# Two-layer fp32 trunk on one core: the split of the weights into high and low parts, done on a whole loaded tile instead of one 128-row chunk

## The chip, the core and the metric

One NeuronCore of a Trainium2 chip runs the whole program in one launch. The metric is device time in microseconds (us); lower is better. The engines named below are PE (the matrix engine; PEld is its weight load, which overlaps it), DVE (the vector engine), ACT (the scalar engine), POOL and SP (whose queue issues most transfers from memory).

## The reference

Two layers over 256 tokens of width 2048, all in fp32. Layer 0 mixes a differential attention with a gated delta rule, layer 1 is a dilated attention, and each is followed by a squared-ReLU MLP. Cut to what matters here:

```python
D_MODEL = 2048
SEQ = 256
D_FF = 4 * D_MODEL
...
def rms_norm(x, g):
    xf = x.astype(jnp.float32)
    y = xf * lax.rsqrt(jnp.mean(xf * xf, axis=-1, keepdims=True) + NORM_EPS)
    return (y * g.astype(jnp.float32)).astype(x.dtype)
...
def squared_relu_mlp(h, w1, w2):
    return jnp.square(jax.nn.relu(h @ w1)) @ w2
...
    proj = h @ w_in
...
    return o @ w_out
```

The time goes into the products with the large weights: `w_in` and `w_out` of both mixers, and `w1` (2048 x 8192) and `w2` (8192 x 2048) of both MLPs.

## The kernel before

**The large products.** `dense()` computes one output block, 256 tokens by up to 512 columns, in two PSUM tiles of 128 tokens. It walks over the contracted dimension in chunks of 128 rows, 16 for a full block. Each operand is held as the sum of a high and a low part, both of the type `F32R`, and each chunk costs three products for each token half: high by high (L206), high by the weights' low part (L207), and low by the weights' high part (L208). That is six matmuls of 128x128 by 128x512 to a chunk.

**The weights' way.** `wload` (L171) has SP's queue load two chunks at once into a raw tile `wr` of 128 x 2 x 512 fp32 (4 buffers). For each chunk ACT copies its half of the raw tile to the high part `wh` (L201, a cast), and DVE subtracts the high part from the raw half to get `wl` (L202, which the profile shows at L107, the line of the helper `tt`). `wh` and `wl` are each 128 x 512 and come from a pool with 6 buffers, so that up to six split chunks exist at a time. A name such as `n_3h<-n_3r` is the high part of block 3 of the product n, made from its raw tile; `n_3l` is the low part.

**What sets the order.** The engines run in order. Which instruction stands where on each engine is decided by a tile scheduler from priorities: an instruction normally has the place in which the program issues it, and `tc.high_priority(offset=AHEAD)` with AHEAD = 60 puts the two instructions of a split 60 places earlier. After a chunk `drip()` takes a step or two of the side work, which lies in three streams of generators: attention and delta rule, norms, transposes.

**The stages.** Layer 0's mixer runs from 0 to about 509 us with products such as b0 to b3 (delta rule inputs), z0 to z2 (gates, 264 columns wide), a and v blocks, and `wo`. MLP 0 follows to about 1216 us, layer 1's mixer (products c and cv; heads' side work e1 to e7) to about 1601 us, then MLP 1. An MLP works in 4 groups. In each it makes four products m_0 to m_3 (x times `w1`), each followed by ReLU and square on ACT, 16 block transposes on DVE (L289), a cast `hh` on ACT (L314) and a subtraction `hl` on DVE, both 128 x 1024. Then come four products n_0 to n_3 with `w2`, which take `hh` and `hl` as stationary operands. So the first chunks of n_0 that need m_3's `hh` and `hl` come twelve chunks after m_3's last matmul, and there are 8 such passages from m_3 to n_0.

**The start.** The first three raw tiles of b0 are loaded between the pieces of x. ACT scales the transposed pieces of x (`xa0h`, L123), DVE makes their low parts (`xa0l`, L113), and b0's first splits stand between these.

## Time and profile before

| | us |
|---|---|
| median of 3 runs | 2316.6 |
| the runs | 2315.55, 2316.6, 2317.71 |
| span of the profiled execution, first to last instruction | 2313.0 |
| PE busy | 2298.6 |
| DVE busy | 1733.1 |
| ACT busy | 1275.1 |

The profiled execution is known by its span, which lies 3.6 us under the median of the runs. A busy time is the sum over the instructions of an engine, so it shows how much of the span an engine was not idle, and neither how fast it worked nor what it waited for. Idle time is listed with what released the engine from it: in a row, `[1.12 <-ACT b0h L201]` says that the engine had been idle for 1.12 us until ACT's instruction on b0h of line 201 ended. A row `x2` is two instructions in a row of the same form, with their joint time. The granted clock of PE was 1.000 of full speed in the whole span.

### The profile page before, as it was taken

What the parts mean: (1) busy time and instruction counts of PE and PEld (TensorE: products, weight loads), DVE (VectorE), ACT (ScalarE), POOL (GpSimd) and SP (SyncE); (2) the same over time, 40 slices, a digit from 0 to 9 for tenths busy, and PEclk for the clock granted to TensorE, in tenths of its full rate; (3) what the DMA queues carried; (4) which work ended last, traced back from release to release, by engine and by line L of the source; (5) the groups of instructions that cost most, each with busy time, mean ns of one, the idle gap of its engine ahead of it and who ended that gap; (6) DMA issues with size and microseconds to landing.
All of it is one profiled execution on the core that took longest, in us unless ns stands there. A gap on an engine that the chain in (4) does not pass through costs nothing.

```text
span 2313.0 us, 31488 instructions
## 1 busy us (share of the span) xinstructions
PE 2298.6 (99%) x10536; PEld 1889.0 (82%) x10536; DVE 1733.1 (75%) x3539; ACT 1275.1 (55%) x2376; POOL 5.6 (0%) x15
## 2 busy tenths in 40 slices
PE   9999999999999999999999999999999999999999
PEld 8888888788888888888888888888888888888887
DVE  7758778867757757857898888987875775775774
ACT  6656665655545545545555555556554554554553
POOL 0000000000000000000000000000000000000000
PEclk9999999999999999999999999999999999999999
DMA  8655454556566666665656555555656656656564
GB/s 264 174 170 166 149 174 143 166 180 190 192 188 183 202 186 186 202 188 186 198 183 200 172 166 176 171 175 181 190 193 189 192 191 190 192 191 189 185 209 155
DMA packets 264775, 426.65 MB, mean 184 GB/s; under 512 B 22514, under 2 KB 94372, under 8 KB 264612
## 3 DMA queue, kind: packets, MB, share of 16 engines
q1 hardware_dynamic: 255812, 420.04, 57.7%
q10 hardware_dynamic: 8800, 4.60, 0.8%
q8 instruction: 82, 1.34, 0.2%
q14 instruction: 81, 0.66, 0.1%
HBM read 420.11 MB, written 4.46 MB: 184 GB/s over the span
## 4 chain that ended last, share of the span: by engine, by line
PE 88%; DVE 8%; DMA 2%; ACT 1%; issue 1%; SPq 0%; ACTq 0%; DVEq 0%
PE n_0p L208 3%; PE n_2p L207 3%; PE n_1p L207 3%; PE n_1p L208 3%; PE n_2p L206 3%; PE n_1p L206 3%; PE n_2p L208 3%; PE n_0p L207 3%; PE n_0p L206 3%; PE n_3p L208 3%; PE n_3p L207 3%; PE n_3p L206 3%; PE m_0p L206 3%; PE m_0p L207 3%; PE m_0p L208 3%; PE m_3p L208 3%
## 5 line engine op out<-in xcount | busy, mean ns | idle before, releaser
L107 DVE TENSOR_TENSOR n_3l<-n_3r,n_3h 128x512 fp32r<-128x512 f32 x128 | 88.5, 692 | 73.0 <-ACT n_3h L201 72.6
L107 DVE TENSOR_TENSOR n_2l<-n_2r,n_2h 128x512 fp32r<-128x512 f32 x128 | 88.4, 692 | 73.0 <-ACT n_2h L201 72.6
L107 DVE TENSOR_TENSOR m_0l<-m_0r,m_0h 128x512 fp32r<-128x512 f32 x128 | 88.5, 692 | 68.0 <-ACT m_0h L201 67.8
L201 ACT CAST n_3h<-n_3r 128x512 fp32r<-128x512 f32 x128 | 79.3, 621 | 94.8 <-PE n_3p L208 59.4
L201 ACT CAST n_2h<-n_2r 128x512 fp32r<-128x512 f32 x128 | 79.3, 620 | 94.8 <-PE n_2p L208 59.4
L107 DVE TENSOR_TENSOR n_1l<-n_1r,n_1h 128x512 fp32r<-128x512 f32 x128 | 87.0, 691 | 55.0 <-ACT n_1h L201 54.8
L201 ACT CAST m_0h<-m_0r 128x512 fp32r<-128x512 f32 x128 | 79.6, 622 | 83.8 <-DVE m_0l L107 39.8
L201 ACT CAST n_1h<-n_1r 128x512 fp32r<-128x512 f32 x128 | 78.6, 620 | 81.7 <-PE n_1p L208 59.4
L201 ACT CAST m_1h<-m_1r 128x512 fp32r<-128x512 f32 x128 | 78.1, 622 | 64.7 <-PE m_1p L208 35.3
L107 DVE TENSOR_TENSOR m_1l<-m_1r,m_1h 128x512 fp32r<-128x512 f32 x128 | 87.1, 691 | 33.7 <-ACT m_1h L201 32.0
L201 ACT CAST n_0h<-n_0r 128x512 fp32r<-128x512 f32 x128 | 77.4, 619 | 48.5 <-PE n_0p L208 37.1
L201 ACT CAST m_3h<-m_3r 128x512 fp32r<-128x512 f32 x128 | 77.1, 621 | 46.8 <-PE m_3p L208 35.3
L201 ACT CAST m_2h<-m_2r 128x512 fp32r<-128x512 f32 x128 | 76.9, 621 | 46.8 <-PE m_2p L208 35.3
L107 DVE TENSOR_TENSOR n_0l<-n_0r,n_0h 128x512 fp32r<-128x512 f32 x128 | 84.9, 689 | 11.3 <-ACT n_0h L201 9.6
L107 DVE TENSOR_TENSOR m_3l<-m_3r,m_3h 128x512 fp32r<-128x512 f32 x128 | 84.9, 689 | 11.3 <-ACT m_3h L201 9.6
L107 DVE TENSOR_TENSOR m_2l<-m_2r,m_2h 128x512 fp32r<-128x512 f32 x128 | 84.9, 689 | 11.2 <-ACT m_2h L201 9.5
L289 DVE STREAM_TRANSPOSE m_0hT<-m_0r 32x256 f32<-32x256 f32 x128 | 55.8, 436 | 10.5 <-ACT m_0r L123 8.0
L289 DVE STREAM_TRANSPOSE m_1hT<-m_1r 32x256 f32<-32x256 f32 x128 | 55.8, 436 | 10.4 <-ACT m_1r L123 7.9
L289 DVE STREAM_TRANSPOSE m_2hT<-m_2r 32x256 f32<-32x256 f32 x128 | 55.8, 436 | 10.4 <-ACT m_2r L123 7.9
L289 DVE STREAM_TRANSPOSE m_3hT<-m_3r 32x256 f32<-32x256 f32 x128 | 55.8, 436 | 10.4 <-ACT m_3r L123 7.9
L208 PE MATMUL n_0p<-n_0h,m_3hl 128*128 128x512 f32 x64 | 25.8, 403 | 0.0
L207 PE MATMUL n_0p<-n_0l,m_2hh 128*128 128x512 f32 x64 | 25.3, 396 | 0.0
(2552 smaller groups left out, 7405.7 us busy)
## 6 DMA issues: line engine op xcount, KB each, us to landing
m_0r<-in_mlp_w_dram SPq DMA_DIRECT2D x64, 512.0 KB
m_1r<-in_mlp_w_dram SPq DMA_DIRECT2D x64, 512.0 KB
m_2r<-in_mlp_w_dram SPq DMA_DIRECT2D x64, 512.0 KB
m_3r<-in_mlp_w_dram SPq DMA_DIRECT2D x64, 512.0 KB
n_0r<-in_mlp_w_dram SPq DMA_DIRECT2D x64, 512.0 KB
n_1r<-in_mlp_w_dram SPq DMA_DIRECT2D x64, 512.0 KB
n_2r<-in_mlp_w_dram SPq DMA_DIRECT2D x64, 512.0 KB
n_3r<-in_mlp_w_dram SPq DMA_DIRECT2D x64, 512.0 KB
```

The source lines that it names most:

```text
L107: V.tensor_tensor(out=o, in0=a, in1=b, op=op)
L201: S.copy(wh, w)
L206: E.matmul(o, lhsT=sh, rhs=wh, start=kc == first, stop=False)
L207: E.matmul(o, lhsT=sh, rhs=wl, start=False, stop=False)
L208: E.matmul(o, lhsT=sl, rhs=wh, start=False, stop=kc == last)
L289: V.transpose(out=dv[:, :, :, q], in_=sv[:, :, :, j, :])
```

## The change

The split of the weights works on the whole raw tile. At every second chunk one ACT cast makes the high part of both chunks, 128 x 2 x 512, and one DVE subtraction the low part; the six matmuls of each chunk read their half of these tiles. `wh` and `wl` have twice the size and half as many buffers (3 instead of 6), so that they take the same memory. The two instructions of a pair stand in the program where those of its first chunk stood, with the same offset of 60. Comments and docstrings are taken out; lines after the split are numbered one higher (L207 to L209 for the matmuls).

```diff
-    wp = ctx.enter_context(tc.tile_pool(name="wp", bufs=6))
+    wp = ctx.enter_context(tc.tile_pool(name="wp", bufs=3))
...
             if j % 2 == 0:
                 raw = pre[j // 2] if j // 2 < len(pre) else wload(wsrc, kc, nm)
-            w = raw[:, j % 2, :n]
-            wh = wp.tile([P, 512], F32R, tag="wh", name=f"{nm}h{kc}")[:, :n]
-            wl = wp.tile([P, 512], F32R, tag="wl", name=f"{nm}l{kc}")[:, :n]
-            with tc.high_priority(offset=AHEAD):
-                S.copy(wh, w)
-                tt(wl, w, wh.bitcast(F32), ALU.subtract)
+                w = raw[:, :, :n]
+                wh2 = wp.tile([P, 2, 512], F32R, tag="wh", name=f"{nm}h{kc}")[:, :, :n]
+                wl2 = wp.tile([P, 2, 512], F32R, tag="wl", name=f"{nm}l{kc}")[:, :, :n]
+                with tc.high_priority(offset=AHEAD):
+                    S.copy(wh2, w)
+                    tt(wl2, w, wh2.bitcast(F32), ALU.subtract)
+            wh, wl = wh2[:, j % 2], wl2[:, j % 2]
             for h in range(NH):
                 sh, sl = stat(kc, h)
                 o = ps[h][:, :n]
```

In the program as built, ACT has 792 instructions fewer and DVE 792 fewer; PE has the same matmuls and transposes, in an order that differs only within layer 0's mixer. Three places follow, before and after; the number at the end of a name tells buffers apart, and the width is at the end of a row.

ACT at the start of the program, before: b0's casts (L201) stand between the activations that scale x's pieces and sum its squares.

```order
L123 ACTIVATE xa0h<-xa0t_132,gt 128x256
L201 CAST b0h_225<-b0r_108 128x512
L201 CAST b0h_235<-b0r_108 128x512
L123 ACTIVATE xa0h<-xa0t_132,gt 128x256
L123 ACTIVATE xa0h<-xa0t_141,gt 128x256
L125 ACTIVATE xas0j_247,ssqp<-xq_100 128x512
L125 ACTIVATE xas1j_269,ssqp<-xq_101 128x512
L123 ACTIVATE xa0h<-xa0t_141,gt 128x256
L201 CAST b0h_249<-b0r_112 128x512
L123 ACTIVATE xa1h<-xa1t_152,gt 128x256
L201 CAST b0h_259<-b0r_112 128x512
```

The same place after:

```order
L123 ACTIVATE xa0h<-xa0t_132,gt 128x256
L201 CAST b0h_225<-b0r_108 128x1024
L123 ACTIVATE xa0h<-xa0t_132,gt 128x256
L123 ACTIVATE xa0h<-xa0t_141,gt 128x256
L125 ACTIVATE xas0j_243,ssqp<-xq_100 128x512
L125 ACTIVATE xas1j_261,ssqp<-xq_101 128x512
L201 CAST b0h_245<-b0r_112 128x1024
L123 ACTIVATE xa0h<-xa0t_141,gt 128x256
L123 ACTIVATE xa1h<-xa1t_152,gt 128x256
```

The first two casts became one, and the second pair's cast now stands ahead of the last piece of `xa0h` and the first of `xa1h`.

DVE around a passage from m_3 to n_0, before (m_0_3 is group 0, block 3; the layer's number is left out): transposes of m_3's result, the subtractions for n_0's weights, and the subtraction `m_0_3hl` that n_0's last chunks need.

```order
L289 STREAM_TRANSPOSE m_0_3hT<-m_0_3r 32x2x4x32 x2
L107 TENSOR_TENSOR n_0_0l_6812<-n_0_0r_6809,n_0_0h_6811 128x512
L289 STREAM_TRANSPOSE m_0_3hT<-m_0_3r 32x2x4x32 x2
L107 TENSOR_TENSOR n_0_0l_6822<-n_0_0r_6809,n_0_0h_6821 128x512
L289 STREAM_TRANSPOSE m_0_3hT<-m_0_3r 32x2x4x32 x3
L107 TENSOR_TENSOR n_0_0l_6834<-n_0_0r_6831,n_0_0h_6833 128x512
L289 STREAM_TRANSPOSE m_0_3hT<-m_0_3r 32x2x4x32 x2
L107 TENSOR_TENSOR n_0_0l_6844<-n_0_0r_6831,n_0_0h_6843 128x512
L107 TENSOR_TENSOR m_0_3hl<-m_0_3hT,m_0_3hh 128x1024
L107 TENSOR_TENSOR n_0_0l_6856<-n_0_0r_6853,n_0_0h_6855 128x512
```

The same place after:

```order
L290 STREAM_TRANSPOSE m_0_3hT<-m_0_3r 32x2x4x32 x4
L107 TENSOR_TENSOR n_0_0l_6012<-n_0_0r_6009,n_0_0h_6011 128x1024
L290 STREAM_TRANSPOSE m_0_3hT<-m_0_3r 32x2x4x32 x5
L107 TENSOR_TENSOR n_0_0l_6034<-n_0_0r_6031,n_0_0h_6033 128x1024
L290 STREAM_TRANSPOSE m_0_3hT<-m_0_3r 32x2x4x32 x4
L107 TENSOR_TENSOR n_0_0l_6056<-n_0_0r_6053,n_0_0h_6055 128x1024
L290 STREAM_TRANSPOSE m_0_3hT<-m_0_3r 32x2x4x32 x3
L107 TENSOR_TENSOR n_0_0l_6074<-n_0_0r_6071,n_0_0h_6073 128x1024
L107 TENSOR_TENSOR m_0_3hl<-m_0_3hT,m_0_3hh 128x1024
L107 TENSOR_TENSOR n_0_0l_6092<-n_0_0r_6089,n_0_0h_6091 128x1024
```

Between two subtractions there are now three to five transposes instead of two or three, and `m_0_3hl` still has one subtraction between it and the last transposes.

ACT in layer 0's mixer during the product z1, before: casts of z1's chunks, 264 columns wide, and the copies `c3x` (L543) of the transposes `c3t` that PE makes for the convolution.

```order
L201 CAST z1h_3243<-z1r_3241 128x264
L201 CAST z1h_3257<-z1r_3241 128x264
L201 CAST z1h_3269<-z1r_3267 128x264
L543 COPY c3x<-c3t_3197 128x2x256
L201 CAST z1h_3292<-z1r_3267 128x264
L123 ACTIVATE qk_3194<-c3x,cw 128x256
L543 COPY c3x<-c3t_3203 128x2x256
```

The same place after:

```order
L201 CAST z1h_2852<-z1r_2850 128x2x264
L201 CAST z1h_2885<-z1r_2883 128x2x264
L201 CAST z1h_2903<-z1r_2901 128x2x264
L544 COPY c3x<-c3t_2865 128x2x256
L544 COPY c3x<-c3t_2871 128x2x256
L123 ACTIVATE qk_2862<-c3x,cw 128x256
L201 CAST z1h_2925<-z1r_2923 128x2x264
```

Three casts, one for each of the three buffers, stand ahead of the copies, and the copies now stand together.

## Rows read from the trace of the kernel before

**Rows 1.** The page's first part: busy time, share of the span and instructions of each engine.

```profile
PE 2298.6 (99%) x10536; PEld 1889.0 (82%) x10536; DVE 1733.1 (75%) x3539; ACT 1275.1 (55%) x2376; POOL 5.6 (0%) x15
```

**Rows 2.** Busy time of each engine by stage: the start, layer 0's mixer, MLP 0, layer 1's mixer, MLP 1. Columns: the stretch, its length, busy us and instructions of each engine, PE's granted clock, share of the DMA engines' time, GB/s.

```profile
0.00:30.00 30.00, 27.20 (x128) 22.32 (x129) 20.07 (x66) 20.98 (x51) 1.20 (x6) 1.00 0.81 264
30.00:460.00 430.00, 426.50 (x2282) 355.85 (x2281) 337.28 (x952) 273.53 (x665) 4.38 (x9) 1.00 0.56 170
...
509.00:1216.00 707.00, 707.00 (x3083) 578.16 (x3082) 521.36 (x893) 372.97 (x608) 0.00 (x0) 1.00 0.61 190
1216.00:1601.00 385.00, 380.58 (x1744) 315.53 (x1743) 326.01 (x748) 216.28 (x416) 0.00 (x0) 1.00 0.55 177
1601.00:2309.00 708.00, 708.00 (x3083) 577.55 (x3081) 494.77 (x830) 362.91 (x580) 0.00 (x0) 1.00 0.60 189
```

**Rows 3.** What PE waited for, over the span: us in total, number of waits, the longest. The first two rows shown are the first and the last of three alike (e3pt, e1pt, e5pt). The last row is the smallest that the view lists.

```profile
PE e3pt L231 <- DVE e3sm L117: 1.5, 1, 1.5
...
PE e5pt L231 <- DVE e5sm L117: 1.5, 1, 1.5
...
PE c3t L231 <- ACT c3x L543: 0.9, 1, 0.9
...
PE g0lp L705 <- DMA g0xy<-scx: 0.2, 1, 0.2
```

**Rows 4.** The timeline in MLP 0, in the product n_3 (first and seventh matmul of the block), around the end of n_2 on ACT and DVE, and in m_2. Columns: start, us, engine, line, operation, out and in, shape, idle before and its releaser.

```profile
664.68 0.40 PE L206 MATMUL n_3p<-n_3h,m_0hh 128*128 128x512 f32 x1
...
666.08 0.40 PE L206 MATMUL n_3p<-n_3h,m_0hh 128*128 128x512 f32 x1
...
735.40 0.39 PE L206 MATMUL m_2p<-m_2h,xb0h 128*128 128x512 f32 x1
...
736.76 0.39 PE L206 MATMUL m_2p<-m_2h,xb1h 128*128 128x512 f32 x1
...
666.28 0.62 ACT L201 CAST n_3h<-n_3r 128x512 fp32r<-128x512 f32 x1 [0.77 <-PE n_3p L208]
...
664.13 0.69 DVE L107 TENSOR_TENSOR n_3l<-n_3r,n_3h 128x512 fp32r<-128x512 f32 x1 [0.71 <-ACT n_3h L201]
```

**Rows 5.** Busy time in two stretches of MLP 0: the products n_1 to n_3 of group 0, and m_1 to m_3 of group 1; each is three blocks of 16 chunks, 288 matmuls. Columns as in rows 2.

```profile
619.88:687.08 67.20, 67.20 (x290) 54.05 (x288) 36.58 (x55) 29.82 (x48) 0.00 (x0) 1.00 0.61 193
708.88:774.16 65.28, 65.28 (x289) 54.07 (x288) 55.96 (x100) 38.18 (x61) 0.00 (x0) 1.00 0.60 187
```

**Rows 6.** Prices of one instruction: two of the page's costliest groups (busy us, mean ns of one, idle before and what ended it), and the 128x1024 cast and subtraction in the views of the tiles m_0hh and m_0hl (duration in ns, least, median and most, first and last start).

```profile
L107 DVE TENSOR_TENSOR n_3l<-n_3r,n_3h 128x512 fp32r<-128x512 f32 x128 | 88.5, 692 | 73.0 <-ACT n_3h L201 72.6
...
L201 ACT CAST n_3h<-n_3r 128x512 fp32r<-128x512 f32 x128 | 79.3, 621 | 94.8 <-PE n_3p L208 59.4
...
L314 ACT CAST m_0hh<-m_0hT x8: 1052/1054/1056, 547.1 to 2169.1; 128x1024 fp32r<-128x1024 f32 x8
...
L107 DVE TENSOR_TENSOR m_0hl<-m_0hT,m_0hh x8: 1225/1226/1226, 548.2 to 2170.1; 128x1024 fp32r<-128x1024 f32 x8
```

**Rows 7.** The timeline of the start, by engine: ACT's first and second casts for b0, the subtractions on DVE that follow them, and PE's first matmuls of b0 and its first on the second pair's low part.

```profile
7.78 1.13 ACT L201 CAST b0h<-b0r 128x512 fp32r<-128x512 f32 x2
...
11.74 0.62 ACT L201 CAST b0h<-b0r 128x512 fp32r<-128x512 f32 x1 [0.50 <-DMA b0r<-in_ab_w_in_dram]
...
8.42 1.29 DVE L107 TENSOR_TENSOR b0l<-b0r,b0h 128x512 fp32r<-128x512 f32 x2
...
8.44 0.73 PE L206 MATMUL b0p<-b0h,xa0h 128*128 128x512 f32 x2 [1.12 <-ACT b0h L201]
9.16 0.50 PE L207 MATMUL b0p<-b0l,xa0h 128*128 128x512 f32 x1
...
13.14 0.50 PE L207 MATMUL b0p<-b0l,xa0h 128*128 128x512 f32 x1 [0.23 <-DVE b0l L107]
```

**Rows 8.** The timeline of the first passage from m_3 to n_0: the cast and the subtraction of m_3's result, the last transposes ahead of them, and PE's first matmul on `m_3hl` with the one after it.

```profile
611.35 0.90 DVE L289 STREAM_TRANSPOSE m_3hT<-m_3r 32x256 f32<-32x256 f32 x2
...
612.28 1.06 ACT L314 CAST m_3hh<-m_3hT 128x1024 fp32r<-128x1024 f32 x1 [2.83 <-DVE m_3hT L289]
...
613.37 1.23 DVE L107 TENSOR_TENSOR m_3hl<-m_3hT,m_3hh 128x1024 fp32r<-128x1024 f32 x1 [0.40 <-ACT m_3hh L314]
...
614.69 0.46 PE L208 MATMUL n_0p<-n_0h,m_3hl 128*128 128x512 f32 x1
614.99 0.39 PE L206 MATMUL n_0p<-n_0h,m_3hh 128*128 128x512 f32 x1
```

**Rows 9.** Layer 1: busy time in the 42 us ahead of PE's wait for `e1sm` (columns as in rows 2), two of the small steps of a Newton iteration in that stretch, and the row of that wait.

```profile
1286.00:1328.00 42.00, 42.00 (x189) 34.87 (x188) 40.92 (x102) 22.44 (x43) 0.00 (x0) 1.00 0.52 165
...
1319.43 0.17 DVE L113 SCALAR_TENSOR_TENSOR e2q<-e2q,e2z 128x8 f32<-128x8 f32 x1
1319.63 0.17 DVE L113 SCALAR_TENSOR_TENSOR e2rs<-e2q,e2rs 128x8 f32<-128x8 f32 x1
...
1330.06 0.70 PE L231 MATMUL e1pt<-ca,e1sm 128*128 128x128 f32 x3 [1.47 <-DVE e1sm L117]
```

**Rows 10.** The timeline during the product z1 in layer 0: a cast on ACT, the copy behind it, and PE's transposes that wait.

```profile
273.04 0.41 ACT L201 CAST z1h<-z1r 128x264 fp32r<-128x264 f32 x1 [1.51 <-PE z1p L208]
273.36 0.58 ACT L543 COPY c3x<-c3t 128x512 f32<-128x512 f32 x1
...
273.99 0.66 PE L231 MATMUL c3t<-ca,b3raw 128*128 128x128 f32 x4 [0.91 <-ACT c3x L543]
```

## The prediction, made before the changed kernel ran

> **What bounds the kernel now.** I read the page's busy times first, then the waits of PE, and then single stretches of the timeline, because a busy share alone does not say which engine the others wait for. PE is busy for 2298.6 of 2313.0 us; DVE for 1733.1 and ACT for 1275.1 [rows 1]. The stages say where PE is not busy: 30.00 - 27.20 = 2.80 us in the first 30 us, 430.00 - 426.50 = 3.50 in layer 0's mixer, 385.00 - 380.58 = 4.42 in layer 1's mixer, and nothing in the two MLPs, where 707 of 707 and 708 of 708 us are busy [rows 2]. The waits name those gaps: three of 1.5 us on DVE in layer 1, the rest under 1 us each down to 0.2 [rows 3], besides PE's first matmul of b0, which waits 1.12 us [rows 7].
>
> Busy could still mean slow, so I looked at a steady place. In n_3 a chunk of six matmuls takes 666.08 - 664.68 = 1.40 us, in m_2 736.76 - 735.40 = 1.36, with no idle time named in these rows [rows 4]. There ACT's cast waits 0.77 us for PE to release a buffer, and DVE's subtraction waits 0.71 us for that cast [rows 4]. So the split follows PE and not the other way: PE is last. Work saved on ACT and DVE is worth something only at the waits of a few tenths to 1.5 us.
>
> **The change part by part.** *What it saves.* Two casts of 621 ns become one of 1054, two subtractions of 692 ns one of 1226 [rows 6]: 2 x 621 - 1054 = 188 ns of ACT and 2 x 692 - 1226 = 158 ns of DVE for each pair. With 792 pairs that is 149 us of ACT and 125 us of DVE. The matmuls are the same, so PE's 2298.6 us stay. I cost this saving at nothing by itself: the cover is PE's 1.36 to 1.40 us per chunk. If the cover were gone, it would be 125 us at most, the part of DVE, but nothing in rows 2 to 4 puts DVE last in an MLP. For the 264-column products I have no row of a double width; between no saving and 158 ns the place is as covered, so it is nothing.
>
> *A later first use.* A large split is ready later than the first of two small ones. At the start this lies on the path. Before, the first cast ends near 8.40 and PE begins at 8.44 [rows 7]. Now it takes 7.78 + 1.05 = 8.83, so PE begins about 8.88; the subtraction starts near 8.85 instead of 8.42, takes 1.23, and PE's first matmul on a low part, at 9.16 before, comes at about 10.12. The two high matmuls that lie between cover none of this 0.96. The second pair's cast waits for its DMA until 11.74 in either version [rows 7]; it then ends at 12.79 and its subtraction at 14.03, so the matmul of 13.14 comes at about 14.08: 0.94 us late. The first delay is therefore not added, it is absorbed in the second. But one group of four small transposes that PE did ahead of 13.14 now comes behind (about 0.35 us), and the fourth pair, loaded last, may cost 0.3: +1.6 us. The ends: +0.4 (only the later first cast, if PE's other work fills the rest) and +2.5 (0.94 twice, with both small items). I take 1.6, since 0.94 rests on a DMA that the row shows to be late anyhow.
>
> *Fewer buffers.* Six chunk buffers become three pairs. Before, a buffer came free at each chunk; now it does at every second. Estimated from rows 4 and 6: the cast of a pair can start when PE is done with the pair three ahead, the chain behind it takes 1.05 + 1.23 = 2.3 us, and PE has two pairs, 4 x 1.40 = 5.6 us, to work on: 3.3 us to spare. In the products m this must hold DVE's transposes too: five at 0.45 (the row of two at 611.35, 0.90 [rows 8]) are 2.2 us, leaving 1.1. So it costs nothing while no further us is lost on DVE; the cost if it is gone stands with the rivals. The raw tiles have the same four buffers; each is freed by one subtraction instead of by the second of two, and SP's queue has the same loads in the same order but for three exchanges. DMA engines stand at 0.55 to 0.61 of their time in the stages [rows 2], so I cost that at nothing.
>
> *The passages from m_3 to n_0.* Before, `m_3hl` starts at 613.37 and runs 1.23 us, and PE's matmul on it, at 614.69, is followed by the next after 0.30 us instead of the 0.23 of a steady chunk: 0.07 lost [rows 8]. Afterwards DVE has four large subtractions in place of eight small ones between the same 16 transposes: 4 x 0.158 = 0.6 us earlier, which is more than 0.07. Eight passages give -0.5 us, with 0 as the other end.
>
> *Layer 1.* DVE is busy for 40.92 of the 42 us ahead of the wait for `e1sm` [rows 9], so here DVE is last and the saving counts. Four pairs ahead of it give -0.6 us. Against that, the small steps of a Newton iteration, which used to alternate with other work, now follow one another more often in the order; one right behind another starts 0.20 us after it [rows 9], and some four that were hidden between large steps now stand so: about +0.8. I take nothing for the three waits, with -0.6 and +0.6 each as ends: -1.8 to +1.8.
>
> *Layer 0's mixer.* Its waits are 3.50 us [rows 2]. The program's order changes there on PE as well. In the product z1, ACT's cast waits 1.51 us for PE, a copy stands behind it, and PE's transposes wait 0.91 us for that copy [rows 10]. Three such casts now stand ahead of the copies, each able to wait longer, but the copies are also together, so PE waits once rather than twice. Nothing else in the rows prices that, so it is bounded by the waits vanishing (-3.5) and doubling (+3.5); I take 0, between them.
>
> **Sum.** 2313.0 + 1.6 - 0.5 + 0 + 0 = 2314.1 us of span. The span stood 3.6 us below the median of the runs, and the same distance gives 2316.6 + 1.1 = 2317.7. All ends together would be 2316.6 + 0.4 - 0.5 - 1.8 - 3.5 = 2311.2 and 2316.6 + 2.5 + 0 + 1.8 + 3.5 = 2324.4. A measurement of this kernel can tell about 0.2% from no change, that is 4.6 us: 2312.0 to 2321.2 counts as the same.
>
> **Rivals.** *A: the relieved engines end the waits.* For it: layer 1's three waits of 1.5 us [rows 3] are on a full DVE [rows 9]. Without all waits after the first 30 us, 3.50 + 4.42 = 7.9 us [rows 2], it would be 2317.7 - 7.9 = 2309.8. Against it: the mean gain before e1 is 0.6, not 1.5 us. Chance 0.06.
>
> *B: ACT's order holds PE.* A cast that waits for a whole pair keeps the small copies behind it on ACT for one chunk longer, and PE's transposes wait for these. It is seen once at 0.91 us [rows 10]; with one more chunk of waiting (0.7 us at half width) and 0.2 us more of cast it is 1.8 us an event. From the second such new event it leaves the band (2317.7 + 3.6 = 2321.3), and three give 2323.1: slower. For it: the order puts three casts ahead of the copies, with three buffers. Against it: the copy's own wait in the row was shorter than the cast's. Chance 0.10.
>
> *C: PE has room, and splits cost it time.* In n a chunk takes 1.40 us, in m 1.36 [rows 4], and three blocks 67.20 against 65.28 [rows 5]. If the many small splits slowed PE in n, the change would bring n to 1.36: 512 chunks x 0.04 = 20.5 us, 2297.2. Against it: DVE works 55.96 us in the faster stretch and only 36.58 in the slower [rows 5], so more work beside PE goes with the faster rate, not with the slower. Chance 0.03.
> The Trainium skill ("Perfetto Trace Analysis", section "Identifying the Most-Contended Engine") warns that PE's matmul busy share is no measure of its headroom, and would have one read the weight loads' busy share instead. By that rule PE stands at 82% [rows 1] and not at 99%, and some of the other 18% could be won, as in C. The waits of ACT and DVE in rows 4 speak against it here: whatever PE's headroom is, more speed on the split does not reach it.
>
> *D: too few buffers in the MLPs.* If DVE lost more than the 1.1 us left beside five transposes, PE would show a gap once in each of the 32 blocks m. At 0.3 us (a small part of a 1.23 us subtraction) that is 10 us: 2327. Against it: DVE has 158 ns less to do for each pair and was idle 65.28 - 55.96 = 9.3 us in three blocks [rows 5]. Chance 0.03.
> The same page of the Trainium skill (section "Optimization Strategy") says that a gap which repeats on the engine that should be full can come from too little room or too few buffers for the next tile. That is D, and no run so far shows it: in rows 2 the MLPs have no idle time on PE.
>
> *E: the change is not what it says.* The order as built shows casts and subtractions of 128x1024 and of 2x264 and 792 instructions fewer on each engine, so the chance is 0.01; the time would be 2316.6.
>
> **How the numbers follow.** The forecast has 0.77. Faster by over 0.2% are A and C, 0.09; slower by over 0.2% are B and D, 0.13; the same are the forecast and E, 0.78. The range 2311 to 2324 takes in the forecast with its unknown costs, E, and B with three events; A, C and D, 0.12, are left out.
>
> **What would show it.** Right: the MLP stages still full of PE with 1.36 and 1.40 us a chunk, DVE's and ACT's busy times down by some 125 and 149 us, PE's first low matmul near 10.1 us and the second pair's near 14.1, 614.69's row at its steady distance, three waits near 1.5 us in layer 1. Wrong: a gap on PE that repeats in the MLPs (D), n's chunks at 1.36 (C), several new waits of PE on ACT's copies in layer 0 (B), or layer 1's waits gone (A). The forecast would also be wrong if the start cost much more than 2.5 us, as it would if the late subtractions kept the first raw tiles from being refilled.

## The result and the profile after

The changed kernel takes 2328.63 us (median of 5 runs, 2326.33 to 2330.96), the kernel before 2316.6. The ratio is 1.005, with a 95% interval of 1.0038 to 1.0062: slower by 12 us, clear of the 0.2% that the measurement can tell, and outside the range of 2311 to 2324. The profiled execution has a span of 2325.6 us against 2313.0.

The page's first part of the changed kernel, which answers to [rows 1]:

```profile
PE 2299.6 (99%) x10536; PEld 1890.9 (81%) x10536; DVE 1649.1 (71%) x2747; ACT 1154.9 (50%) x1584; POOL 5.6 (0%) x15
```

PE has the same work, DVE 84.0 us less and ACT 120.2 us less. The busy time of the stages after, in the columns of [rows 2]:

```profile
0.00:30.00 30.00, 25.71 (x118) 21.15 (x119) 18.31 (x53) 20.84 (x43) 1.20 (x6) 0.94 0.78 262
30.00:460.00 430.00, 417.86 (x2238) 347.64 (x2237) 319.75 (x808) 252.67 (x530) 4.38 (x9) 1.00 0.55 162
460.00:509.00 49.00, 48.06 (x217) 38.59 (x216) 30.80 (x46) 24.17 (x34) 0.00 (x0) 1.00 0.63 196
509.00:1216.00 707.00, 707.00 (x3090) 579.16 (x3089) 489.03 (x633) 333.96 (x357) 0.00 (x0) 1.00 0.63 190
1216.00:1601.00 385.00, 380.07 (x1732) 314.03 (x1731) 316.75 (x620) 191.77 (x281) 0.00 (x0) 1.00 0.57 176
```

The last MLP is left out here; it is full of PE in both kernels. The loss stands in the first three rows: PE is idle for 430.00 - 417.86 = 12.14 us in layer 0's mixer, where it was 3.50, for 0.94 us in the stretch behind it, where it was none, and for 4.29 us in the start, where it was 2.80. Behind these rows PE is idle as little as before. PE's waits name the places (compare [rows 3]):

```profile
PE b0p L207 <- ACT b0h L201: 2.5, 1, 2.5
PE g2lp L706 <- DMA g2xy<-scx: 2.4, 1, 2.4
PE g3lp L706 <- DMA g3xy<-scx: 2.1, 1, 2.1
PE g0lp L706 <- DMA g0xy<-scx: 1.5, 1, 1.5
PE e1pt L232 <- DVE e1sm L117: 1.5, 1, 1.5
...
PE g3po L764 <- DVE d3mx L887: 1.4, 1, 1.4
PE g1lp L706 <- DMA g1xy<-scx: 1.3, 1, 1.3
PE d2s L885 <- DVE g3am L107: 1.2, 1, 1.2
PE d3ot L232 <- DVE d3o L117: 0.9, 1, 0.9
PE g0kt L232 <- DVE g0kh L117: 0.7, 1, 0.7
```

The largest new group is the four waits g0lp to g3lp, 7.3 us together against 0.2 before. They belong to the delta rule, one for each pair of its heads (the function `gdn`, a stream of side work). It inverts small triangular blocks by a chain: PE and DVE make a matrix `m`, ACT's queue writes it out and reads its 16x16 blocks back, some twenty small steps on DVE invert them (from `g2xc<-g2mb` to the copy `g2xc<-g2xc`), ACT's queue writes the result out (`scx`) and reads it back (`xy`), and PE multiplies by it in `lp`. In the stretch of PE's order where `lp` stands, the large product around it cannot go on without it. From 30 us to the end of the mixer PE is idle for 13.1 us instead of 3.5; 7.1 of these 9.6 us more are at the four `lp`, and the copy that `c3t` waited for [rows 3] is not waited for any more.

Two views of the first part of the start, PE's first matmuls with the first cast and subtraction (compare [rows 7]), and the busy time with PE's granted clock by stretches of 2 us (columns as above; the clock is the eighth figure, ahead of the DMA share):

```profile
8.40 1.03 ACT L201 CAST b0h<-b0r 128x1024 fp32r<-128x1024 f32 x1
...
9.46 1.23 DVE L107 TENSOR_TENSOR b0l<-b0r,b0h 128x1024 fp32r<-128x1024 f32 x1 [0.45 <-ACT b0h L201]
...
9.48 0.94 PE L207 MATMUL b0p<-b0h,xa0h 128*128 128x512 f32 x2 [2.52 <-ACT b0h L201]
10.74 0.79 PE L208 MATMUL b0p<-b0l,xa0h 128*128 128x512 f32 x1 [0.32 <-DVE b0l L107]
```

```profile
8.00:10.00 2.00, 0.52 (x2) 0.30 (x2) 1.02 (x2) 2.00 (x6) 0.00 (x0) 0.96 1.05 367
10.00:12.00 2.00, 1.68 (x4) 1.05 (x4) 1.48 (x3) 2.00 (x6) 0.00 (x0) 0.50 1.05 373
12.00:14.00 2.00, 2.00 (x9) 1.68 (x8) 1.64 (x3) 1.42 (x4) 0.00 (x0) 0.69 1.07 397
```

From the first cast to the first matmul on a low part it is now 2.34 us; it was 1.38. In this execution x landed 0.62 us later as well, which is why the cast itself starts at 8.40. After its idle 2.52 us PE runs at the lower of its two clocks (0.50, 1.2 GHz) for some 3 us.

In the MLPs nothing moved. Timeline of PE and DVE at the end of the passage to n_0, and of PE one chunk apart in n_3 and in m_2 (compare [rows 4] and [rows 8]):

```profile
626.01 1.22 DVE L107 TENSOR_TENSOR m_3hl<-m_3hT,m_3hh 128x1024 fp32r<-128x1024 f32 x1
...
628.07 0.39 PE L209 MATMUL n_0p<-n_0h,m_3hl 128*128 128x512 f32 x1
628.30 0.39 PE L207 MATMUL n_0p<-n_0h,m_3hh 128*128 128x512 f32 x1
...
677.80 0.40 PE L207 MATMUL n_3p<-n_3h,m_0hh 128*128 128x512 f32 x1
...
679.19 0.40 PE L207 MATMUL n_3p<-n_3h,m_0hh 128*128 128x512 f32 x1
...
748.39 0.39 PE L207 MATMUL m_2p<-m_2h,xb0h 128*128 128x512 f32 x1
...
749.75 0.39 PE L207 MATMUL m_2p<-m_2h,xb1h 128*128 128x512 f32 x1
```

`m_3hl` is now ready 0.8 us ahead of its matmul and nothing is lost there; six matmuls take 1.39 us in n and 1.36 in m, against 1.40 and 1.36 before.

### The profile page after: what moved, and what is told of

Its sections match the earlier page's. It is cut to its first block, busy times and chain, and to the rows that moved or that the text cites. A ratio compares the mean times of both kernels' runs of the same rounds, so it can differ in the third digit from the quotient of the medians.

```text
span 2325.6 us, 29118 instructions
## 1 busy us (share of the span) xinstructions
PE 2299.6 (99%) x10536; PEld 1890.9 (81%) x10536; DVE 1649.1 (71%) x2747; ACT 1154.9 (50%) x1584; POOL 5.6 (0%) x15
## 4 chain that ended last, share of the span: by engine, by line
PE 86%; DVE 8%; DMA 3%; issue 2%; ACT 1%; ACTq 0%; SPq 0%; DVEq 0%
PE n_1p L209 3%; PE n_2p L209 3%; PE n_2p L208 3%; PE n_0p L207 3%; PE n_1p L207 3%; PE n_0p L208 3%; PE n_1p L208 3%; PE n_0p L209 3%; PE n_2p L207 3%; PE n_3p L207 3%; PE n_3p L209 3%; PE n_3p L208 3%; PE m_0p L207 3%; PE m_0p L209 2%; PE m_3p L209 2%; PE m_0p L208 2%
## 5 line engine op out<-in xcount | busy, mean ns | idle before, releaser
L107 DVE TENSOR_TENSOR n_3l<-n_3r,n_3h 128x1024 fp32r<-128x1024 f32 x64 | 78.4, 1225 | 81.2 <-ACT n_3h L201 81.1
L107 DVE TENSOR_TENSOR n_2l<-n_2r,n_2h 128x1024 fp32r<-128x1024 f32 x64 | 78.4, 1225 | 81.1 <-ACT n_2h L201 81.0
L107 DVE TENSOR_TENSOR m_0l<-m_0r,m_0h 128x1024 fp32r<-128x1024 f32 x64 | 78.4, 1225 | 77.2 <-ACT m_0h L201 77.2
L107 DVE TENSOR_TENSOR n_1l<-n_1r,n_1h 128x1024 fp32r<-128x1024 f32 x64 | 78.4, 1225 | 74.5 <-ACT n_1h L201 74.4
L201 ACT CAST n_3h<-n_3r 128x1024 fp32r<-128x1024 f32 x64 | 67.2, 1049 | 105.1 <-PE n_3p L209 64.2
L201 ACT CAST n_2h<-n_2r 128x1024 fp32r<-128x1024 f32 x64 | 67.1, 1049 | 105.0 <-PE n_2p L209 64.3
L201 ACT CAST n_1h<-n_1r 128x1024 fp32r<-128x1024 f32 x64 | 67.2, 1049 | 100.2 <-PE n_1p L209 64.4
L201 ACT CAST m_0h<-m_0r 128x1024 fp32r<-128x1024 f32 x64 | 67.3, 1052 | 91.0 <-PE m_0p L209 55.0
L107 DVE TENSOR_TENSOR m_1l<-m_1r,m_1h 128x1024 fp32r<-128x1024 f32 x64 | 78.4, 1225 | 36.8 <-ACT m_1h L201 35.8
L201 ACT CAST m_1h<-m_1r 128x1024 fp32r<-128x1024 f32 x64 | 67.5, 1054 | 66.5 <-PE m_1p L209 38.3
L201 ACT CAST n_0h<-n_0r 128x1024 fp32r<-128x1024 f32 x64 | 67.3, 1051 | 59.6 <-PE n_0p L209 27.9
L107 DVE TENSOR_TENSOR m_3l<-m_3r,m_3h 128x1024 fp32r<-128x1024 f32 x64 | 78.4, 1225 | 25.8 <-ACT m_3h L201 24.0
L107 DVE TENSOR_TENSOR n_0l<-n_0r,n_0h 128x1024 fp32r<-128x1024 f32 x64 | 78.4, 1225 | 25.7 <-ACT n_0h L201 24.0
L107 DVE TENSOR_TENSOR m_2l<-m_2r,m_2h 128x1024 fp32r<-128x1024 f32 x64 | 78.4, 1225 | 25.7 <-ACT m_2h L201 24.0
L201 ACT CAST m_3h<-m_3r 128x1024 fp32r<-128x1024 f32 x64 | 67.5, 1054 | 57.4 <-PE m_3p L209 39.9
L201 ACT CAST m_2h<-m_2r 128x1024 fp32r<-128x1024 f32 x64 | 67.5, 1054 | 57.3 <-PE m_2p L209 40.0
L209 PE MATMUL n_1p<-n_1h,m_0hl 128*128 128x512 f32 x64 | 25.3, 396 | 0.0
L209 PE MATMUL n_2p<-n_2h,m_3hl 128*128 128x512 f32 x64 | 25.3, 396 | 0.0
```

Source lines behind the costliest of these rows:

```text
L107: V.tensor_tensor(out=o, in0=a, in1=b, op=op)
L201: S.copy(wh2, w)
L209: E.matmul(o, lhsT=sl, rhs=wh, start=False, stop=kc == last)
```

## The experiments

Layer 0's mixer ends when m_0 begins, at 509.41 us before and 522.80 after: 13.4 us later. The whole span is 12.6 us longer, so everything behind that mixer takes 0.8 us less: MLP 0 0.6 us less, layer 1 1.4 us more (from n_3's last matmul to the next m_0, 385.5 before and 386.9 after), and the rest 1.5 less. In what follows "start" is how much later than before b0's last matmul begins (33.79 before, 36.02 after), and "past the start" is the rest of the delay at the end of the mixer. "Inverse" is the time of the four stretches of DVE from the first to the last step of the inverse, g0 to g3 together, by the timeline. They are, before and after (columns as in [rows 2]):

```profile
106.69:118.31 11.62, 11.62 (x57) 9.71 (x55) 11.62 (x34) 6.31 (x12) 0.00 (x0) 1.00 0.46 136
196.21:205.86 9.65, 9.65 (x52) 7.88 (x51) 9.46 (x32) 5.37 (x14) 0.00 (x0) 1.00 0.52 165
293.49:306.28 12.79, 12.79 (x64) 10.73 (x63) 12.10 (x33) 5.46 (x9) 0.95 (x1) 1.00 0.63 196
384.40:394.54 10.14, 9.69 (x52) 7.41 (x52) 10.00 (x33) 6.16 (x16) 0.00 (x0) 1.00 0.48 155
```

```profile
108.62:122.21 13.59, 13.31 (x65) 10.96 (x64) 13.59 (x33) 6.93 (x10) 0.00 (x0) 1.00 0.51 152
199.75:211.17 11.42, 11.42 (x60) 9.38 (x59) 10.46 (x33) 7.66 (x17) 0.00 (x0) 1.00 0.52 146
297.63:312.13 14.50, 14.50 (x71) 12.15 (x70) 13.11 (x31) 4.80 (x5) 0.95 (x1) 1.00 0.60 174
394.91:404.84 9.93, 8.44 (x42) 6.34 (x43) 9.76 (x32) 5.40 (x13) 0.00 (x0) 1.00 0.33 106
```

The sums are 44.2 and 49.4 us. All runs in one table; times are medians, the ratio is to runs of the kernel before on the same chip.

| kernel | us | ratio (95%) | start | past the start | inverse |
|---|---|---|---|---|---|
| before | 2316.6 | 1 | 0 | 0 | 44.2 |
| changed | 2328.6 | 1.005 (1.0038-1.0062) | 2.2 | 11.2 | 49.4 |
| pair_buffers_only | 2322.4 | 1.0024 (1.0013-1.0036) | 0.9 | 3.9 | 43.4 |
| wide_cast_only | 2334.0 | 1.0078 (1.0063-1.0093) | 1.6 | 6.5 | 45.5 |
| wide_sub_only | 2327.6 | 1.0054 (1.0039-1.0069) | 2.4 | 9.1 | 50.1 |
| narrow_in_layer0 | 2324.7 | 1.004 (1.0026-1.0053) | 1.6 | 3.7 | 44.4 |
| narrow_layer0_sp_first | 2302.3 | 0.994 (0.9925-0.9955) | 2.4 | 3.4 | 44.0 |
| before_sp_first | 2301.1 | 0.9936 (0.9921-0.995) | 0.0 | 0.4 | 43.9 |
| after_ahead30 | 2333.7 | 1.0077 (1.0062-1.0092) | 2.8 | 14.8 | 49.7 |
| after_ahead80 | 2327.7 | 1.0051 (1.0036-1.0066) | 2.8 | 10.8 | 48.7 |
| after_ahead110 | 2331.9 | 1.007 (1.0055-1.0085) | 4.8 | 13.6 | 48.9 |
| before_ahead45 | 2322.4 | 1.0026 (1.0015-1.0037) | 2.5 | 8.3 | 43.5 |
| before_ahead80 | 2321.9 | 1.0024 (1.0015-1.0033) | 2.5 | 1.5 | 44.3 |
| before_lp_later | 2330.0 | 1.0055 (1.0038-1.0072) | 2.8 | 15.6 | 42.8 |
| before_lp_earlier | 2323.7 | 1.0026 (1.0015-1.0036) | 2.2 | 7.6 | 48.8 |
| after_lp_later | 2329.1 | 1.0051 (1.0036-1.0066) | 2.1 | 14.5 | 47.2 |

In the two kernels with narrow splits in layer 0, five transposes of x stand ahead of m_0 that come behind it in the others; their last matmul of the mixer is 2.3 and 2.1 us later past the start. A seventeenth kernel, four_pairs_two_raw, took 2645.9 us (1.1429, 1.141 to 1.1448) and is told below.

The last three columns are of one execution each, and two comparisons say how far to trust them. The kernels before_lp_earlier and before_lp_later start with the same instructions on PE, ACT and DVE as the kernel before, and their starts are 2.2 and 2.8 us late. And narrow_layer0_sp_first has the mixer's order of before_sp_first but for those five transposes and the first splits for m_0; the two differ by 2.4 us in the start and by 3.0 past it (1.7 by the mixer's last matmul). So a difference of 2 or 3 us in these columns shows nothing by itself; the 11.2 us are clear of it.

**The parts of the change, one at a time.** The first three kernels keep the three pair tiles. The first splits each chunk by itself, at its own place:

```diff
-                with tc.high_priority(offset=AHEAD):
-                    S.copy(wh2, w)
-                    tt(wl2, w, wh2.bitcast(F32), ALU.subtract)
             wh, wl = wh2[:, j % 2], wl2[:, j % 2]
+            with tc.high_priority(offset=AHEAD):
+                S.copy(wh, w[:, j % 2])
+                tt(wl, w[:, j % 2], wh.bitcast(F32), ALU.subtract)
```

> High and low parts lie in three pair tiles as in the changed kernel, but each chunk is cast and subtracted by itself, 128x512, at its own place. Theory 1 (the loss of some 10 us in layer 0's mixer comes from the buffers: a cast waits until PE has left a whole pair, DVE's subtraction behind it waits too, and the delta rule's small steps queue behind both): about as slow as the changed kernel, 2325 to 2329 us, with PE's waits for g0lp to g3lp at 1.3 us or more each, and the start about 2 us faster than the changed kernel's. Theory 2 (the loss comes from the width: a small step waits for a 1.23 us subtraction where it waited for one of 0.69): near the kernel before, 2315 to 2319, waits for the four lp under 0.5 us each.

The second keeps the wide cast and subtracts by chunks:

```diff
                     S.copy(wh2, w)
-                    tt(wl2, w, wh2.bitcast(F32), ALU.subtract)
             wh, wl = wh2[:, j % 2], wl2[:, j % 2]
+            with tc.high_priority(offset=AHEAD):
+                tt(wl, w[:, j % 2], wh.bitcast(F32), ALU.subtract)
```

> One wide cast for each pair on ACT, two 128x512 subtractions on DVE, each at its own chunk's place; three pair tiles. Theory 1 (buffers): 2325 to 2329, as the changed kernel. Theory 2 (width of the subtraction on DVE): 2316 to 2320, with only the start's 2 us left of the loss. If the width of the cast on ACT is what counts, 2325 to 2329 here and near 2317 with the wide subtraction alone.

The third casts by chunks, both casts at the pair's place, and subtracts wide:

```diff
-                    S.copy(wh2, w)
+                    S.copy(wh2[:, 0], w[:, 0])
+                    S.copy(wh2[:, 1], w[:, 1])
                     tt(wl2, w, wh2.bitcast(F32), ALU.subtract)
```

> Two 128x512 casts on ACT, both at the pair's place, and one wide subtraction on DVE; three pair tiles. Theory 1 (buffers): 2325 to 2329. Theory 2 (width on DVE): the same 2325 to 2329, and this kernel is told from theory 1 by the other two. A result near 2317 would put the loss on the wide cast. The first matmul of b0 should come some 0.4 us sooner after the first cast starts than in the changed kernel, since it needs one half only.

The totals fit neither theory: 2322.4 with pair buffers alone lies between the two. They are no measure of the mixer's loss either, since layer 1 takes 4.6 us more with pair buffers alone (390.1 against 385.5), 12.7 more with the wide cast and 1.8 with the wide subtraction. The first matmul of b0 came 0.65 us after the first cast began with the wide subtraction alone and 1.08 in the changed kernel, as expected. Past the start, the parts nearly add up: 3.9 us for the pair buffers, 6.5 - 3.9 = 2.6 more with the wide cast, 9.1 - 3.9 = 5.2 more with the wide subtraction, together 11.7 where the whole change has 11.2. With some 2 us of difference between executions, that they add up can be luck. It is with the wide subtraction that the inverse is long, 50.1 us instead of 43.4, and that three of the four lp wait for 3.1 us together, where pair buffers alone have 0.9. The rows of PE's waits for lp, pair buffers alone first, then the wide subtraction:

```profile
PE g3lp L706 <- DVE d2mx L887: 0.5, 1, 0.5
...
PE g2lp L706 <- DMA g2xy<-scx: 0.4, 1, 0.4
```

```profile
PE g1lp L707 <- DMA g1xy<-scx: 1.5, 1, 1.5
...
PE g0lp L707 <- DMA g0xy<-scx: 1.0, 1, 1.0
...
PE g3lp L707 <- DVE d2mx L888: 0.6, 1, 0.6
```

The wide cast alone is the slowest of the three for another reason: the 12.7 us in layer 1, where PE's waits for e1sm, e3sm and e5sm grow from 1.5 to 3.4 us each (1.9 with pair buffers alone). In the changed kernel they stay at 1.5.

How the inverse gets longer is seen in the changed kernel's g2, in the timeline of ACT, DVE and PE; the first step of the inverse is `g2xc<-g2mb,ca`:

```profile
301.74 1.05 ACT L201 CAST a1h<-a1r 128x1024 fp32r<-128x1024 f32 x1 [2.57 <-PE a1p L209]
...
297.63 0.40 DVE L113 SCALAR_TENSOR_TENSOR g2xc<-g2mb,ca 32x256 f32<-32x256 f32 x1
297.96 1.21 DVE L113 SCALAR_TENSOR_TENSOR qk<-c3x,qk 128x1024 f32<-128x1024 f32 x1
...
301.42 0.16 DVE L107 TENSOR_TENSOR g2tm<-g2mb,g2xc 32x12 f32<-32x12 f32 x1
302.83 1.23 DVE L107 TENSOR_TENSOR a1l<-a1r,a1h 128x1024 fp32r<-128x1024 f32 x1 [1.25 <-ACT a1h L201]
303.97 0.15 DVE L107 TENSOR_TENSOR g2xc<-g2tm,g2xc 32x12 f32<-32x12 f32 x1
...
322.23 0.94 PE L706 MATMUL g2lp<-g2xy,g2mT 128*128 128x128 f32 x6 [2.44 <-DMA g2xy<-scx]
```

A step of 0.16 us at 301.42 is followed by a subtraction that waits 1.25 us for its cast, which waits for PE to leave a pair; then it runs 1.23 us, and the next step of the inverse, which needed nothing but the step before, starts at 303.97, 2.55 us after it. PE waits for that chain at 322.23.

That is the place which shows it best, but the subtractions do not hold DVE longer over the four stretches. Counted from each instruction's start to the next one's, less idle time, 21 narrow subtractions take 12.6 us in the kernel before and 11 wide ones 12.5 after. The inverse's own 80 steps take 23.6 and 24.0 us. What grows is other side work between the steps, from 23 instructions and 7.0 us to 32 and 10.4, and DVE's idle time, from 1.0 us to 2.5. One such instruction is `qk` at 297.96, 1.21 us long; in the kernel before it ends ahead of the first step:

```profile
292.35 1.23 DVE L113 SCALAR_TENSOR_TENSOR qk<-c3x,qk 128x1024 f32<-128x1024 f32 x1 [0.46 <-ACT c3x L123]
293.49 0.41 DVE L113 SCALAR_TENSOR_TENSOR g2xc<-g2mb,ca 32x256 f32<-32x256 f32 x1
```

So the chain is longer because other work stands in it and because it waits for casts, not because a wide subtraction takes longer than the narrow ones that it replaces.

**Where the pairs do no harm.** Layer 0's mixer got narrow splits and six chunk buffers from a pool of its own, everything behind it the pairs (the branch in `dense()` that chooses is left out):

```diff
...
+        split.update(wide=False, pool=mix.enter_context(tc.tile_pool(name="wn", bufs=6)))
         mp = mix.enter_context(tc.tile_pool(name="mp", bufs=1))
...
+    split.update(wide=True, pool=ctx.enter_context(tc.tile_pool(name="ww", bufs=3)))
     cb = []
```

> Layer 0's mixer splits each chunk by itself with six chunk buffers, as before; both MLPs and layer 1 split whole pairs with three pair buffers. If the whole loss lies in layer 0's mixer (start, delta rule, end of the mixer), the time is that of the kernel before to within 2 us, 2314 to 2318, with PE idle 3 to 4 us in layer 0 from 30 us on, as before, and layer 1 about 0.5 us shorter. If the pairs cost something in the MLPs that the stages' busy time hides, it is 2320 or more.

It took 2324.7, but not from the splits: the new pools lie behind another one in memory, so the split weights moved by 128 bytes within 512 (read from the addresses in the programs as built; in the changed kernel they lie as before). The 96 matmuls of a block m then took 22.07 us from first to last instead of 21.53, those of n 21.53 instead of 22.07 to 22.17, and the products of the two mixers slowed too. So that the comparison is free of that, the small pool `sp` was allocated first, in this kernel and in the kernel before:

```diff
+    sp = ctx.enter_context(tc.tile_pool(name="sp", bufs=2))
     wp = ctx.enter_context(tc.tile_pool(name="wp", bufs=6))
     xp = ctx.enter_context(tc.tile_pool(name="xp", bufs=4))
-    sp = ctx.enter_context(tc.tile_pool(name="sp", bufs=2))
```

> The kernel before with one pool of small tiles allocated ahead of the weights' pool instead of behind the x tiles'; no instruction changes. Rival C of the prediction (n slower than m because of the splits' number) against an effect of addresses: in the first run with narrow splits in layer 0, the split weights' tiles lay 128 bytes off, and m's blocks of 96 matmuls became 0.55 us slower and n's 0.64 us faster. Here the weights' tiles, the x tiles and the MLP's hidden tiles all lie at the same place within 512 bytes. By the address theory n's chunks take 1.36 us instead of 1.40 and the 32 blocks n give 32 x 0.64 = 20.5 us: 2294 to 2300. By rival C nothing changes: 2314 to 2319.

> Chunk splits in layer 0's mixer and pair splits elsewhere, as in the run with narrow splits in layer 0, and the pool order of the run before this one, so that the split weights' tiles are not moved against the others within 512 bytes. If the pairs are harmless outside layer 0's mixer, it is within 2 us of the run with the kernel before in that pool order, near 2296 by the address theory. If the pairs cost something in the MLPs, it is 4 us or more above that run.

2301.1 and 2302.3 us: with the addresses equal, pairs outside layer 0's mixer leave the time as it is within the intervals, and the loss lies in that mixer. In the traces the two MLPs are 4.1 us shorter with pairs and layer 1 is 1.4 longer. Both kernels are quicker than the two of this study. In before_sp_first six matmuls of n take 1.36 us, as those of m do:

```profile
664.29 0.39 PE L206 MATMUL n_3p<-n_3h,m_0hh 128*128 128x512 f32 x1
...
665.65 0.39 PE L206 MATMUL n_3p<-n_3h,m_0hh 128*128 128x512 f32 x1
```

It gained 15.6 us and not the 20.5 expected. The 24 blocks n_1 to n_3 became 14.5 us shorter, from 22.07 to 22.17 us each to 21.53. The eight blocks n_0 stayed at 22.05, as PE now waits in each of them for `m_3hl` (1.8 us in eight waits, and the matmuls behind a wait start slower); with the pairs of narrow_layer0_sp_first they take 21.53 too.

**Earlier or later places, more buffers.** The splits' place of the changed kernel, and four pair buffers with two raw tiles:

```diff
-AHEAD = 60
+AHEAD = 30
```

> The changed kernel with the splits put 30 places ahead instead of 60. Each wide cast and subtraction stands later in its queue, so it waits less for PE to leave a pair, and fewer small steps of the delta rule stand behind a waiting subtraction. Theory 1 (small steps are held behind splits that wait for a pair buffer): most of layer 0's loss after the start goes, 2317 to 2321, with PE's waits for the four lp under 1 us each. Theory 2 (width of the subtraction alone, 1.23 us in a queue): the loss stays, 2325 to 2330. If the splits come too late for PE, new waits of PE on splits in the MLPs show it and the time is above 2330.

```diff
-    wp = ctx.enter_context(tc.tile_pool(name="wp", bufs=3))
+    wp = ctx.enter_context(tc.tile_pool(name="wp", bufs=4))
...
-        raw = wp.tile([P, 2, 512], F32, tag="wr", name=f"{nm}r{k0}", bufs=4)
+        raw = wp.tile([P, 2, 512], F32, tag="wr", name=f"{nm}r{k0}", bufs=2)
```

> The changed kernel with four pair buffers for the high and low parts and two raw tiles instead of four, so that the memory stays the same. Theory 1 (waiting for pair buffers): the casts find a buffer one pair sooner, so the waits of PE for the four lp fall by most of their 7 us, and layer 0's mixer after the start loses 2 to 4 us instead of 11; 2318 to 2323 in all if two raw tiles are enough for the loads. Theory 2 (width): layer 0 loses as much as in the changed kernel, 2326 to 2331. If two raw tiles starve the casts, ACT's casts wait for DMA in the MLPs and the time is above 2335.

At 30 places the lp of g0 and g1 no longer wait, but PE waits 2.7 us for a cast of av1 and 1.8 us for subtractions of cv1, cv2 and cv3 each: the wide splits now come too late, though in the two mixers and not in the MLPs. The lp of g2 and g3 still wait 1.3 and 2.0 us. Theory 1 got no support, but it is not refuted either: the late splits hide what it would have given back. Two raw tiles starve the casts (ACT waits 343 us for loads between 520 and 1200 us, in MLP 0), so that run tells nothing about buffers.

**Is the side chain late, or is everything shifted?** One more or one less step of the stream between the inverse and lp:

```diff
-            for _ in range(4):
+            for _ in range(5):
                 yield
             for li, b in enumerate(LEVELS):
```

> The changed kernel with one more step (two chunks of a large product, some 2.7 us of PE) between the delta rule's inverse and the first product lp that reads it; nothing else changes. If PE's waits for g0lp to g3lp (1.5, 1.3, 2.4 and 2.1 us) are a side chain that arrives late by just that much, they fall to near zero and the time is 4 to 7 us lower, 2321 to 2325, less what the later end of the chain costs in the mixer's tail. If they come from something that moves along with PE, such as a queue that PE itself holds up, they stay and the time is that of the changed kernel or longer, 2327 to 2333.

> The same extra step in the kernel before, where PE's waits for the four lp are 0.2 us together. It tells what the step costs by itself: nothing if the mixer's tail has room (2315 to 2318), up to 4 us if the delta rule's last head sets the end of the mixer.

> The kernel before with one step less ahead of lp, so that PE reaches it some 2.7 us sooner. If the chain arrived just in time (no slack), PE waits about 2 us at each of the four lp and the time is 4 to 9 us longer, 2320 to 2326. If the chain had more than 2.7 us of slack, nothing changes, and a chain stretched by 1 to 2 us could not have cost the changed kernel 7 us.

The extra step took the waits for lp from 7.3 us to 1.7 (g0 alone) in the changed kernel, and won nothing: 2329.1. The waits went elsewhere: PE is idle for 12.0 us from 30 us to the end of the mixer instead of 13.1, now at other steps of the side work (`d1t` 1.9, `d2po` 1.3, `g1pa` and `g3pa` 1.1 each). In the kernel before the same step costs 13 us, where at most 4 were expected, and one step less costs 7. With one step less, two of the four lp wait (g2lp 0.9 us, g3lp 1.1), where about 2 us at each were expected. PE's largest waits past the start with one step less are spread over many products:

```profile
PE a1p L207 <- DVE a1l L107: 1.2, 1, 1.2
PE g3lp L705 <- DMA g3xy<-scx: 1.1, 1, 1.1
PE g0ly L711 <- DVE g0P L107: 1.1, 1, 1.1
```

So the interleaving of layer 0's mixer before the change is one that fits, and both moves of it cost. The last four runs moved the splits' place in both kernels:

> The changed kernel with its splits 80 places ahead instead of 60. Theory M (layer 0's mixer has an interleaving of PE, DVE and ACT that fits the narrow splits with no slack, so that any shift costs; wide splits can be fitted too): the time moves by several us, and could fall to 2315 to 2322. Theory W (a wide subtraction on DVE stretches the delta rule's chain wherever it stands): 2325 to 2332, and the four stretches of DVE from the first to the last step of the inverse stay near 49 us together, where the kernel before has 44.

> The changed kernel with its splits 110 places ahead. Theories as for 80 places: M, several us up or down from 2328.6; W, 2325 to 2332 again with the inverse's stretches near 49 us. If the earlier place only makes each split wait longer for its buffer at the head of its queue, slower: above 2332.

> The kernel before with its narrow splits 45 places ahead instead of 60. Theory M: layer 0's mixer loses 3 to 12 us, as it did with the delta rule's lp one step earlier or later, and the rest of the program nothing: 2319 to 2329. Theory W: narrow splits are robust against their place, 2315 to 2319.

> The kernel before with its narrow splits 80 places ahead. Theory M: 2319 to 2329, with the loss in layer 0's mixer. Theory W: 2315 to 2319.

Narrow splits lose past the start 8.3 us at 45 places, nothing at 60 and 1.5 at 80 (in the quickest of ten executions, 2318.75 us; their median is 2321.9, within theory M's range). Wide ones lose 14.8, 11.2, 10.8 and 13.6 at 30, 60, 80 and 110. Theory M is right that the place matters and that 60 was a good one for narrow splits; it is wrong that wide ones can be fitted by their place, at least by these four. Theory W is right on the length of the inverse: 48.7 to 50.1 us in the five kernels whose subtraction is wide with lp in its place, 43.4 to 45.5 in those where it is narrow. It is not right on the reason, as the shares of DVE's time above show, and it does not explain all 11 us. before_lp_earlier has 48.8 us of inverse with narrow splits, since 28 subtractions instead of 21 then fall into it, so a long inverse is not the mark of width.

## Why the prediction was wrong

**The step that failed** is the one on layer 0's mixer: "Nothing else in the rows prices that, so it is bounded by the waits vanishing (-3.5) and doubling (+3.5); I take 0, between them." Measured, it is +11.2 us. The bound was taken from the waits that existed, and a place that did not wait was taken for one that could not. The row that pointed at it was the wait for g0lp, the smallest of the list at 0.2 us [rows 3]: a chain of side work that arrives just as PE needs it. A wait of 0.2 us looks like a place with nothing to lose; it was one with nothing to spare. Three more of its kind do not show in a list of waits at all, and they had little to spare: before, their lp begin 9.2 to 9.5 us after the inverse's end without a wait; after, 9.0 to 10.1 us after it, with PE waiting at each. The landing of the data between the two is not in the trace, so the room itself cannot be read.

**What the mechanism was.** Rival B had its half: a small step stands behind a split that waits for PE to leave a pair. It was placed on ACT's copies at z1, where the wait of 0.9 us even went away, and missed the inverse on DVE. Shown are: the loss lies in layer 0's mixer (with the whole change, pairs elsewhere are free); PE spends it waiting, 9.6 of the 11.2 us, most of it for the delta rule's side work; with the wide subtraction the inverse takes about 5 us more, by other work and waits between its steps; relieving the waits for lp alone wins nothing, and the other moves of that interleaving cost 1.5 to 15.6 us with narrow splits. How the 11.2 us divide between the width, the pair buffers and the retiming stays open: the parts add up to 11.7 us, but each of them also moves the places of others, and no run changed the width and kept the order. More pair buffers, the direct test of theory 1, have no clean run.

**The start.** Forecast +1.6, measured 2.2 by b0's end, of which 0.62 is x's later landing in this execution. That the sum is close is luck as far as the runs show. One term of it held: the first matmul on a low part came 0.96 us later after the first cast, as worked out (2.34 - 1.38). The second step was otherwise than forecast: the second pair's low part made PE wait no more, but PE ran at half its clock from about 10 to 13 us. That is no mark of the wide cast: narrow_layer0_sp_first, with the start's order unchanged, waited 2.2 us for its first cast, had a granted clock of 0.89 in the first 30 us, and was 2.4 us late as well, and so were before_lp_earlier and before_lp_later (2.2 and 2.8). The kernel before was profiled in an execution with a quick start, so how much of the 2.2 us belongs to the change is not shown.

**The saving.** 125 us of DVE and 149 of ACT were forecast; 84.0 and 120.2 were measured. The term took each instruction's own duration, 692 and 621 ns; in a full queue the next one starts before the last has ended (two subtractions in a row take 1.29 us together [rows 7], not 1.38), and that overlap was counted as work to be saved. It changed nothing in the sum, since the saving was priced at nothing, and that was right: the MLPs have no idle PE before or after.

**What held.** The passages to n_0 gave their 0.07 us each back. Layer 1's three waits stayed at 1.5 us; the stage took 1.4 us more, inside the range given for it. Too few buffers in the MLPs (D) did not show; the Trainium skill ("Perfetto Trace Analysis", section "Optimization Strategy") says that a gap which repeats on the engine that should be full can come from too little room or too few buffers. Here PE's idle time in the stretch of MLP 0 is 0 of 707 us with three pairs as with six chunks. Rival C had the right number for a wrong reason: n's chunks can take 1.36 us, but by the place of their tiles, not by fewer splits.

## What to carry to other kernels

Where an engine's queue is shared by bulk work and a latency chain of small steps, widening the bulk instructions saves busy time but changes what stands between the steps, and here that cost more than it saved; look for the chain's slack, which a list of waits does not show when it is just zero. A stage in which PE is full from end to end (the MLPs here, 2.2 us shorter together) hardly cares about the width; a stage that is held together by a fitted interleaving should be left out of the change, or be fitted again if that can be done: four places of the wide splits did not do it here. To find such a stage beforehand, move one step of it by one place on the chip: here that cost 7 to 13 us before any change was made. And profile more than one execution before a difference of 2 us is explained.

## What the runs showed of the hardware

A matmul's spacing depended on where its operands lie relative to each other. With the split weights and the stationary tiles at the same place within 512 bytes, 96 matmuls of 128x512 took 21.53 us, with 128 bytes between them 22.07 to 22.17, in the MLP's products where PE waited for nothing (before, changed, narrow_in_layer0, before_sp_first, narrow_layer0_sp_first) and whichever of the two was moved. Between the kernel before and before_sp_first the order of the instructions on PE, DVE and ACT is the same. No other distance than 0 and 128 bytes was seen. Allocating one small pool first gave 0.64% (2301.1 against 2316.7 us, interval 0.9921 to 0.995) without touching an instruction.

PE's granted clock fell to 0.50, the lower of its two levels, at the start of the 14 executions in which PE had been idle for 1.95 to 3.04 us at a stretch ahead of its first large product, and in wide_sub_only, where 1.39 us of idle time were soon followed by another 1.05. It did not where PE was idle for 1.12 us (the kernel before) and 1.66 us (before_sp_first).
